# Modulation sums by ScalarE products and adding transfers, and a twentieth pair of FFN tiles by seven products

## The chip, the cores and the metric

One core of one Trainium2 chip. The metric is the device time of one execution in microseconds (us). Before the change three runs gave 699.42, 699.88 and 700.14; the median is 699.88.

## The reference, cut to what matters

One decoder layer in float32, sequence 512, width 1024. A conditioning vector c gives six modulation vectors, and two sublayers are each put back by a LayerNorm:

```python
c_act = silu(c)
mod = c_act @ ada_w + ada_b                       # [1024] x [1024, 6144]
sh1, sc1, g1, sh2, sc2, g2 = split(mod, 6)
h = x * (1 + sc1) + sh1
y = hybrid_mixer(h, ...)   # 8 attention heads and 16 SSD heads, one input and one output projection
x = layer_norm(ALPHA * x + (1 + g1) * y, ln1_g, ln1_b)
h = x * (1 + sc2) + sh2
u = causal_dwconv(h @ w_up, conv_w, conv_b)       # [512,1024] x [1024, 5632], conv of 3 taps
g, val = split(u, 2)
y = (silu(g) * val) @ w_down                      # [512,2816] x [2816,1024]
x = layer_norm(ALPHA * x + (1 + g2) * y, ln2_g, ln2_b)
```

## The kernel before, in words

The work is recorded by a list scheduler that lies in the kernel itself (class `Order`). Each piece of the layer is a Python generator, a "thread", that yields instructions, buffer requests (`Alloc`) and conditions (`Need`). `Order.run` holds a clock for each engine, prices each instruction (`price`), and always issues the instruction that could start first; among those that could start at nearly the same time, that of the thread with the lower priority number goes first. What it decides is only an order: on the chip each engine runs its own list strictly in order, and each instruction waits on semaphores for what it reads. A price or a delay (`late`) in the scheduler so changes no instruction, only where it stands. The engines are called PE (TensorE), DVE (VectorE, `V`), ACT (ScalarE, `A`), POOL (GpSimd, `G`), SP (SyncE, `S`, which issues the plain transfers); `GD` are transfers issued by POOL, which can add into their destination (`accum_op`).

**Products.** All products are float32 made of three fp32r products (high*high, high*low, low*high; `mm3`). Weights are loaded in 512 KB items (`raw`, by `w_load`), split by `w_split` into high and low parts (ACT copies `wh`, DVE subtracts to get `wl`), and used by `products()` in the order of the list `items`: input projection (tiles `fm`, `tm`), output projection (`po`, two halves of 512 columns), up projection of the FFN (`up` and `sP`), down projection (`dn`). `w_next` counts the items taken in `wpos[0]` and marks `("item", i)`; other threads start on that mark.

**Pairs of up tiles.** The up projection has 22 pairs of 128-column tiles (gate and value of one channel group). The first four tiles (pairs 0 and 1) are made in two halves of the sequence, since the first half is there sooner. A pair in the list `SEVEN` (line 695; pairs 3 to 21) is made by `seven(j)`: seven products of half-size blocks in place of eight, each of 12 matmuls of 256 columns, into two banks `sP`. `split_seven` makes its seven split weight blocks `wq` (DVE also sums two blocks, `sw`), `sums_seven` makes two of the sums by adding transfers on POOL (`raw<-raw`, `sw<-in_ffn_up_w`), and `seven_out` adds parts back on ACT and DVE. `quarters` makes the four sums `ts` of the activations that they need. Pair 2 is a plain pair: 48 matmuls of 512 columns.

**Modulation.** The first two of the six vectors (sh1, sc1) are made at the start. `ada_mid` makes g1 (`ada_row`, kept as a row in 128 partitions, used by `ln1`), then sc2 and sh2 (`ada_cols`, kept in `mcol`, used by `ln1_t`). `ada_last` makes g2 for the last LayerNorm. Each of the three in `ada_mid` calls `ada_acc`: eight loads `ad` of 128 rows of ada_w (512 KB each), each multiplied by a column of silu(c) (`csil`) and summed on DVE into `acc`, one load at the mark of one item. Then `ada_half` splits a half of `acc` (`acch`, `accl`) and sums it over the partitions by two matmuls (`pad`) with ones.

**The scan.** `dt_chain` writes the cumulated decays to DRAM (`drcs`), and `ssd_decay` reads them back for each of eight column tiles as a broadcast `csb` (512 KB, line 943 on). From it ACT makes `er` (exp of a 64x384 part, twice); POOL cuts the upper triangle (`affine_select`); ACT takes eight exps with a bias; DVE multiplies with the scores `sc`. PE reads the result in `py` (`ssd_out`); `ssd_state` makes states (`pst` on PE, `st` on ACT and DVE) and reads them by `pyo`.

**First LayerNorm.** `ln1` takes a 128-row tile of `po`, multiplies by g1 (`yp`), adds x (`xr`), takes statistics (`st`, `mv`; POOL takes the power -0.5), and scales to `XN`; `ln1_t` transposes it on PE (`pt`), applies `mcol` on ACT (`hk`) and splits to `h2h`, `h2l`.

All helpers record through line 309, so every row of the profile names L309; rows are told apart by their tiles.

## Time and profile before

| | |
|---|---|
| median of 3 runs | 699.88 us (699.42 to 700.14) |
| span of the profiled execution, first to last instruction | 698.53 us |
| what lies around the span (median less span) | 1.35 us |
| PE busy | 684.3 us, 98% |
| DVE busy | 607.3 us, 87% |
| ACT busy | 387.8 us, 56% |
| POOL busy | 103.4 us, 15% |
| granted TensorE clock, mean | 0.997 |
| transfers issued by SP, by POOL | 105.93 MB, 9.96 MB |

The page gives no time of its own for the profiled execution beside its span, so the span with the 1.35 us around it is taken for the median. A row of a timeline gives start, duration, engine, operation, `out<-in`, shape, count, and in brackets how long the engine had been idle and what ended that. Matmuls are pipelined and their ends are modelled: a 512-column matmul is drawn 0.39 us long and the next one starts about 0.23 us after it, so PE can be "busy" and still hide a wait of some 0.16 us.

### The profile page before, as it was taken

Reading aid. Unit: us, or ns where it says so; the run is one execution under the profiler, and the core shown is the slowest. Engines: PE = TensorE matmul, PEld = TensorE weight load, DVE = VectorE, ACT = ScalarE, POOL = GpSimd, SP = SyncE. Lnnn points to the kernel's source line nnn. Section 1 sums busy time; section 2 is a strip of 40 time slices with the busy share of each in tenths; the row PEclk is TensorE's granted clock in tenths of the full one; section 3 lists DMA queues with packets and bytes.
Section 4 is the critical chain, followed back from the end, with each engine's and each line's share of the span. In section 5 each row is a group of like instructions: output and inputs, shape, how many; then the busy total and the mean of one; then the engine's idle time right before and its main releaser. Section 6 shows DMA issues by size and latency. Waiting matters only on the chain.

```text
span 698.5 us, 11597 instructions
## 1 busy us (share of the span) xinstructions
PE 684.3 (98%) x4305; PEld 598.0 (86%) x4305; DVE 607.3 (87%) x1119; ACT 387.8 (56%) x739; POOL 103.4 (15%) x109
## 2 busy tenths in 40 slices
PE   8999999999999999999999999999999999999995
PEld 7787877888888888887898999999999998888885
DVE  5888989899999999889999999999999997357646
ACT  2437568845667545313886777777777776111300
POOL 0010021101000000000121121112222005910023
PEclk9999999999999999999999999999999999999998
DMA  8997074134455626677493787877897576232202
GB/s 269 308 289 241 16 215 149 37 87 126 120 178 160 237 92 212 246 275 256 137 233 73 174 200 165 187 174 167 189 204 173 130 255 220 94 108 70 91 30 92
DMA packets 134924, 116.64 MB, mean 167 GB/s; under 512 B 4565, under 2 KB 113489, under 8 KB 134867
## 3 DMA queue, kind: packets, MB, share of 16 engines
q1 hardware_dynamic: 122099, 105.93, 49.4%
q0 software_dynamic: 12768, 9.96, 9.8%
q8 instruction: 34, 0.56, 0.3%
q14 instruction: 23, 0.19, 0.1%
HBM read 106.66 MB, written 4.23 MB: 159 GB/s over the span
## 4 chain that ended last, share of the span: by engine, by line
PE 85%; DVE 6%; DMA 4%; SPq 3%; ACT 1%; issue 1%; POOL 0%; DVEq 0%; ACTq 0%; POOLq 0%
PE sP L309 27%; PE fm L309 18%; PE dn L309 18%; PE po L309 7%; PE first L309 3%; SPq L309 3%; PE tm L309 2%; PE psS L309 2%; PE pov L309 1%; PE pT L309 1%; PE py L309 1%; DMA csb<-drcs 1%; PE pyo L309 1%; PE up L309 1%; DMA raw<-in_ffn_up_w_dram 1%
## 5 line engine op out<-in xcount | busy, mean ns | idle before, releaser
L309 PE MATMUL sP<-ts,wq 128*128 128x256 f32 x912 | 113.9, 281 | 0.0
L309 DVE TENSOR_TENSOR wl<-raw,wh 128x1024 fp32r<-128x1024 f32 x64 | 80.6, 1265 | 36.6 <-ACT wh L309 36.1
L309 ACT ACTIVATE wh<-raw 128x1024 fp32r<-128x1024 f32 x64 | 67.3, 1055 | 78.0 <-PE dn L309 31.1
L309 PEld LDWEIGHTS sP<-ts,wq 128*128 128x128 f32 x912 | 110.4, 189 | 0.0
L309 PE MATMUL dn<-wh,mid 128*128 128x512 f32 (+1 forms) x356 | 102.7, 371 | 0.0
L309 PE MATMUL sP<-h2h,wq 128*128 128x256 f32 x456 | 87.2, 281 | 0.0
L309 PEld LDWEIGHTS dn<-wh,mid 128*128 128x128 f32 x356 | 64.7, 188 | 12.6
L309 PEld LDWEIGHTS sP<-h2h,wq 128*128 128x128 f32 x456 | 72.7, 189 | 0.0
L309 PE MATMUL fm<-hh,wh 128*128 128x512 f32 x176 | 72.6, 412 | 0.0
L309 PE MATMUL fm<-hh,wl 128*128 128x512 f32 x176 | 69.4, 394 | 0.0
L309 PE MATMUL fm<-hl,wh 128*128 128x512 f32 x176 | 69.4, 394 | 0.0
L309 PE MATMUL dn<-wl,mid 128*128 128x512 f32 (+1 forms) x178 | 66.1, 372 | 0.0
L309 PE MATMUL sP<-h2l,wq 128*128 128x256 f32 x228 | 64.0, 281 | 0.0
L309 DVE TENSOR_TENSOR wq<-raw,wq 128x512 fp32r<-128x512 f32 x76 | 50.8, 686 | 0.7
L309 ACT ACTIVATE wq<-raw 128x512 fp32r<-128x512 f32 x76 | 45.3, 623 | 0.0
L309 ACT ACTIVATE c<-sP 128x256 f32<-128x256 f32 x76 | 29.0, 382 | 28.5 <-PE sP L309 28.2
L309 PEld LDWEIGHTS sP<-h2l,wq 128*128 128x128 f32 x228 | 43.1, 189 | 0.1
L309 PE MATMUL po<-wh,os 128*128 128x512 f32 x128 | 42.1, 396 | 0.0
L309 PEld LDWEIGHTS fm<-hh,wl 128*128 128x128 f32 x176 | 33.1, 188 | 7.7
L309 PEld LDWEIGHTS fm<-hh,wh 128*128 128x128 f32 x176 | 33.2, 189 | 7.0 <-issue 0.7
L309 DVE TENSOR_TENSOR wq<-sw,wq 128x512 fp32r<-128x512 f32 x57 | 38.8, 684 | 0.0
L309 PEld LDWEIGHTS dn<-wl,mid 128*128 128x128 f32 x178 | 33.5, 188 | 6.2
(264 smaller groups left out, 1489.9 us busy)
## 6 DMA issues: line engine op xcount, KB each, us to landing
raw<-in_ffn_up_w_dram SPq DMA_DIRECT2D x44, 512.0 KB, 4.5
raw<-in_mix_in_w_dram SPq DMA_DIRECT2D x26, 512.0 KB, 5.8
ad<-in_ada_w_dram SPq DMA_DIRECT2D x24, 512.0 KB, 3.9
raw<-in_ffn_down_w_dram SPq DMA_DIRECT2D x22, 512.0 KB, 3.7
aw<-in_ada_w_dram SPq DMA_DIRECT2D x32, 256.0 KB, 5.8
raw<-in_mix_out_w_dram SPq DMA_DIRECT2D x12, 512.0 KB, 4.0
sw<-in_ffn_up_w_dram SPq DMA_DIRECT2D x19, 256.0 KB, 4.9
raw<-raw POOLq DMA_DIRECT2D x19, 256.0 KB, 4.6
```

What stands on the lines that cost most here:

```text
L309: getattr(self.hw[op.eng], op.fn)(*op.args, **op.kw)
```

## The change

- **Twentieth pair.** `SEVEN` begins at 2: pair 2 is made by seven products too.
- **Modulation sums.** In `ada_acc` the DVE multiply-adds go. ACT multiplies each load by its column of `csil` in place (the first one into `acc`), and seven adding transfers by POOL sum them into `acc`. This holds for g1, sc2 and sh2; `ada_last` still sums on DVE.
- **Loads ahead.** A thread `ada_load` of its own issues the 24 loads, up to two ahead of their use.
- **Priorities.** `ada_mid` goes from 3 (past item 16; 8 before that) to 1.9 (past item 8); `ada_last` goes from 8 to 2.6 eight items before the up projection.
- **Scheduler's prices.** A `csb` transfer counts as landing 1.0 us later for its readers; the 64x384 exp, the reciprocal and a large `affine_select` get other prices. Only the order follows from these.
- **A shared tile.** `OA` can be allocated by either of two attention threads.

```diff
-        self.regs[t.tensor.name].late = 2.0 if a.name == "ad" else 0.0
+        self.regs[t.tensor.name].late = {"ad": 2.0, "csb": 1.0}.get(a.name, 0.0)
...
-            return 0.04 + 0.00093 * n + (0.06 + 0.07 * ptr if ptr else 0) + (0.09 if "accum_out" in kw else 0)
+            return 0.04 + (0.0013 if outs[0].shape[0] == 64 and n == 384 else 0.00093) * n + (0.06 + 0.07 * ptr if ptr else 0) + (0.09 if "accum_out" in kw else 0)
...
-                return 0.065 + 0.0065 * n
+                return 0.15 + 0.0065 * n
...
-            return 0.06 + 0.001 * n + (0.5 if n > 512 else 0)
+            return 0.06 + 0.001 * n
...
-    SEVEN = list(range(3, 22))
+    SEVEN = list(range(2, 22))
...
-        if j % 2 == 0:
-            OA[j] = yield buf("e", [P, 2, 2, SEQ], "oa", dt=F32R)
+        if j - j % 2 not in OA:
+            OA[j - j % 2] = None
+            OA[j - j % 2] = yield buf("e", [P, 2, 2, SEQ], "oa", dt=F32R)
+            R.mark(("OA", j - j % 2))
+        yield Need(("OA", j - j % 2))
...
-    def ada_acc(idx, item):
+    ADQ = {}
+
+    def ada_load():
+        for idx, item in ((2, ADA0), (4, ADA1), (3, ADA2)):
+            for kc in range(KC):
+                yield Need(("item", item + kc))
+                aw = yield buf("b", [P, DM], "ad", "adraw")
+                yield S.dma_start(aw, ada[kc * P:(kc + 1) * P, idx * DM:(idx + 1) * DM])
+                ADQ[idx, kc] = aw
+                R.mark(("ad", idx, kc))
+
+    def ada_acc(idx):
         acc = yield buf("b", [P, DM], "acc")
         for kc in range(KC):
-            yield Need(("item", item + kc))
-            aw = yield buf("b", [P, DM], "ad", "adraw")
-            yield S.dma_start(aw, ada[kc * P:(kc + 1) * P, idx * DM:(idx + 1) * DM])
+            yield Need(("ad", idx, kc))
+            aw = ADQ.pop((idx, kc))
             if kc == 0:
-                yield V.tensor_scalar(acc, aw, csil[:, 0:1], None, op0=OP.mult)
+                yield A.activation(acc, aw, AF.Copy, scale=csil[:, 0:1])
             else:
-                yield V.scalar_tensor_tensor(acc, aw, csil[:, kc:kc + 1], acc, op0=OP.mult, op1=OP.add)
+                yield A.activation(aw, aw, AF.Copy, scale=csil[:, kc:kc + 1])
+                yield GD.dma_start(acc, aw, accum_op=OP.add)
             R.free(aw)
...
-    R.spawn(ada_mid(), lambda: 3 if wpos[0] > 16 else 8)
+    R.spawn(ada_mid(), lambda: 1.9 if wpos[0] > 8 else 8)
+    R.spawn(ada_load(), 4)
...
-    R.spawn(ada_last(), 8)
+    R.spawn(ada_last(), lambda: 2.6 if wpos[0] > UP0 - 8 else 8)
```

The lists of the engines differ from the start of the scan up to the start of the pairs by seven products; ahead of that and through the down projection they stand as before. Three places follow, each before and after the change.

ACT at the start of the scan, before: from the copy `csT` that feeds the decays' way through DRAM on. `wh` are weight copies, `Y` and `th` belong to the convolution, `er` and `csb` read the broadcast decays.

```order
L309 ACTIVATE csT_939<-pcs_929 64x128
...
L309 ACTIVATE th_951<-Y_659 128x512
L309 ACTIVATE wh_967<-raw_666 128x1024
L309 ACTIVATE er_985<-csb_962 64x384 x2
L309 ACTIVATE th_1010<-Y_659 128x512
L309 ACTIVATE er_987<-csb_963 64x384 x2
L309 ACTIVATE st_990<-pst_1021 128x128
L309 ACTIVATE wh_1023<-raw_809 128x1024
L309 ACTIVATE er_992<-csb_964 64x384 x2
L309 ACTIVATE csb_962<-csb_962,ncs_86 128x128 x8
```

The same engine and place after the change; `ad` is a product of the modulation, in place.

```order
L309 ACTIVATE csT_940<-pcs_930 64x128
...
L309 ACTIVATE th_952<-Y_659 128x512
L309 ACTIVATE wh_974<-raw_666 128x1024
L309 ACTIVATE ad_954<-ad_954,csil_75 128x1024
L309 ACTIVATE th_1016<-Y_659 128x512
L309 ACTIVATE wh_1024<-raw_809 128x1024
L309 ACTIVATE er_988<-csb_965 64x384 x2
L309 ACTIVATE er_990<-csb_966 64x384 x2
L309 ACTIVATE csb_965<-csb_965,ncs_86 128x128 x8
```

The product `ad`, the second `th` and the second `wh` now stand ahead of the first `er`; the copy `st` has left ACT (it is a copy on DVE now), and the first eight exps come after two `er` and not three.

POOL in the same stage, before: the triangle cuts of the column tiles.

```order
L309 AFFINE_SELECT csb_962<-csb_962 128x1024
L309 AFFINE_SELECT csb_963<-csb_963 128x1024
L309 AFFINE_SELECT csb_964<-csb_964 128x1024
L309 AFFINE_SELECT csb_1155<-csb_1155 128x1024
L309 AFFINE_SELECT csb_1193<-csb_1193 128x1024
```

And after; `DMA acc<-ad` are the adding transfers of the first modulation sum.

```order
L309 DMA acc_804<-ad_954 128x1024
L309 AFFINE_SELECT csb_965<-csb_965 128x1024
L309 AFFINE_SELECT csb_966<-csb_966 128x1024
L309 AFFINE_SELECT csb_967<-csb_967 128x1024
L309 DMA acc_804<-ad_1021 128x1024
L309 AFFINE_SELECT csb_1142<-csb_1142 128x1024
L309 AFFINE_SELECT csb_1177<-csb_1177 128x1024
L309 DMA acc_804<-ad_1104 128x1024
L309 AFFINE_SELECT csb_1248<-csb_1248 128x1024
```

Each adding transfer waits at the head of POOL's list for its product and for the landing of the one before it, and the cuts behind it wait with it.

DVE at the first tile of the first LayerNorm, before: from the product with g1 on. The rows `ISA junk` and `ISA col` are the column sums of sh2.

```order
L309 SCALAR_TENSOR_TENSOR acc_2836<-ad_3179,csil_75,acc_2836 128x1024
L309 TENSOR_TENSOR yp_3285<-po_3139,row_2286 128x512
L309 SCALAR_TENSOR_TENSOR xr_3031<-xr_3031,yp_3285 128x512
L309 BN_STATS st_3107<-xr_3031 128x6
L309 BN_AGGR mv_3108<-st_3107 128x2
L309 TENSOR_SCALAR mv_3108<-mv_3108 128x1
L309 ISA junk_3212,col_3211<-pad_3287,ident_68 128x128
...
L309 ISA col_3211 128x1
L309 SCALAR_TENSOR_TENSOR mv_3108<-mv_3108 128x1
```

And after:

```order
L309 SCALAR_TENSOR_TENSOR acc_2921<-ad_3256,csil_75,acc_2921 128x1024 x2
L309 TENSOR_TENSOR yp_3327<-po_3201,row_1678 128x512
L309 SCALAR_TENSOR_TENSOR xr_3098<-xr_3098,yp_3327 128x512
L309 BN_STATS st_3166<-xr_3098 128x6
L309 BN_AGGR mv_3167<-st_3166 128x2
L309 TENSOR_SCALAR mv_3167<-mv_3167 128x1
L309 TENSOR_TENSOR accl_3323<-acc_2921,acch_3322 128x512
L309 SCALAR_TENSOR_TENSOR mv_3167<-mv_3167 128x1
L309 TENSOR_SCALAR XN_3360<-xr_3098,mv_3167 128x512
```

Between the statistics and the scaling to `XN` one subtraction stands where the eight rows of the column sums stood; those come earlier now.

More of the change, by code (lines that the diff above doesn't have):

```diff
@@ L1107, in ada_half, with ada_row @@
         return pa
-    def ada_row(idx, key, res, item):
-        acc = yield from ada_acc(idx, item)
+    def ada_row(idx, key, res):
+        acc = yield from ada_acc(idx)
         row = yield buf("b", [P, DM], "row")
@@ L1122, in ada_cols @@
     def ada_cols():
-        for idx, item in ((4, ADA1), (3, ADA2)):
-            acc = yield from ada_acc(idx, item)
+        for idx in (4, 3):
+            acc = yield from ada_acc(idx)
             col = yield buf("t", [P, 8], "col")
@@ L1150, in ada_mid @@
         yield Need(("item", 2))
-        yield from ada_row(2, "g1p", ROWS, ADA0)
+        yield from ada_row(2, "g1p", ROWS)
         yield from ada_cols()
```

## The prediction

> **What bounds the kernel now.** I read the page first, then the busy time by stages, then the chain of waits and the timelines of the places where PE stands still. The page:
>
> ```profile
> span 698.5 us, 11597 instructions
> PE 684.3 (98%) x4305; PEld 598.0 (86%) x4305; DVE 607.3 (87%) x1119; ACT 387.8 (56%) x739; POOL 103.4 (15%) x109
> ```
>
> PE is busy for 98% of the span, so time can go in two ways only: less work on PE, or less idle time of PE. The stages show where it is idle (columns: PE, PEld, DVE, ACT, POOL busy, granted clock, DMA share, GB/s):
>
> ```profile
> core 0: us, PE busy (x) PEld busy (x) DVE busy (x) ACT busy (x) POOL busy (x), PEclk, DMA share, GB/s
> 0.00:20.00 20.00, 16.84 (x102) 14.91 (x103) 12.16 (x34) 6.57 (x12) 0.75 (x7) 1.00 0.93 273
> 20.00:40.00 20.00, 18.82 (x93) 14.61 (x92) 17.77 (x50) 8.03 (x14) 0.00 (x0) 1.00 1.11 314
> 40.00:60.00 20.00, 19.62 (x99) 15.15 (x99) 16.06 (x36) 11.74 (x17) 3.81 (x14) 1.00 0.97 309
> ...
> 80.00:100.00 20.00, 19.15 (x92) 15.16 (x91) 17.43 (x41) 10.50 (x20) 1.75 (x2) 1.00 0.51 152
> 100.00:120.00 20.00, 19.51 (x142) 15.61 (x140) 17.64 (x30) 17.71 (x50) 5.19 (x4) 1.00 0.53 166
> 120.00:320.00 200.00, 199.99 (x1134) 164.16 (x1133) 184.62 (x395) 107.79 (x223) 9.81 (x15) 1.00 0.50 162
> 320.00:340.00 20.00, 19.28 (x92) 15.35 (x91) 18.93 (x45) 11.19 (x25) 1.41 (x2) 1.00 0.52 176
> 340.00:380.00 40.00, 40.00 (x281) 37.06 (x280) 37.94 (x62) 30.91 (x55) 7.83 (x8) 1.00 0.73 171
> 500.00:520.00 20.00, 20.00 (x172) 20.00 (x171) 19.82 (x34) 14.82 (x29) 4.37 (x4) 1.00 0.83 186
> ```
>
> The first 60 us lose 4.7 us to the start loads, which the change does not touch; nor does it reorder the down projection and the tail. In between PE is idle for 0.85 and 0.49 us at the scan's start (80 to 120), 0.01 us from 120 to 320, and 0.72 us at the first LayerNorm (320 to 340): 2.07 us in all. That is everything a better order can give back. The chain that ended last says the same of the long stage:
>
> ```profile
> 380.76 187.56 PE sP L309 x1587
> 568.32 122.87 PE dn L309 x594
> ```
>
> Pairs by seven products run on PE without a break, 187.56 us for 1587 matmuls, though DVE is 99% busy beside them (19.82 of 20).
>
> **The change part by part.** *Twentieth pair.* The plain pair 2 lies between these starts:
>
> ```profile
> 367.64 0.40 PE L309 MATMUL up<-h2h,wh 128*128 128x512 f32 x1
> ...
> 378.80 0.28 PE L309 MATMUL sP<-h2h,wq 128*128 128x256 f32 x1
> ```
>
> Its 48 matmuls take 378.80 - 367.64 = 11.16 us. A pair by seven is 84 matmuls at 187.56/1587 = 118.2 ns, 9.93 us. Gain 1.23 us, on PE itself. Its cover: the activations' sums `ts` and the first blocks `wq` must be ready 11 us sooner than now.
>
> ```profile
> 350.50 1.04 PE L309 MATMUL pt<-ident,XN 128*128 128x128 f32 x8
> ...
> 364.13 0.69 DVE L309 TENSOR_TENSOR ts<-d,ts 128x512 fp32r<-128x512 f32 x1
> ...
> 368.98 0.68 DVE L309 TENSOR_TENSOR wq<-raw,wq 128x512 fp32r<-128x512 f32 x1
> ```
>
> PE gets from its last transposes (350.50) to the new pair's place in 17.1 us, and `ts` is done 14.3 us after them (364.8): 2.8 us of slack. The first `wq` now ends at 369.7, too late, but the new list of DVE has it and three more ahead of the `ts` rows; four operations of about 0.6 us apart eat most of the 2.8 us, and the subtractions of the plain pair that go and the modulation work that DVE loses give it back. I take 0, with 0 to 1 us lost as the bounds.
>
> *Modulation sums.* What DVE loses and ACT gains:
>
> ```profile
> L309 DVE SCALAR_TENSOR_TENSOR acc<-ad,csil,acc 128x1024 f32<-128x1024 f32 x28 | 35.7, 1280 | 0.3 <-DMA ad<-in_ada_w_dram 0.2
> L309 DVE TENSOR_SCALAR acc<-ad,csil 128x1024 f32<-128x1024 f32 x4 | 3.0, 745 | 0.0
> L309 ACT ACTIVATE wh<-raw 128x1024 fp32r<-128x1024 f32 x64 | 67.3, 1055 | 78.0 <-PE dn L309 31.1 <-DVE raw L309 23.3 <-PE po L309 15.7
> ```
>
> DVE is rid of 21 x 1.28 + 3 x 0.745 = 29.1 us; ACT gets 24 operations of the size of `wh`, 25.3 us. Nearly all of it lies between 85 and 300, where PE is idle for 0.01 us from 120 on: a freer DVE can give nothing there, and the 25 us on ACT cost nothing as long as it is not last (107.79 of 200 busy). At 100 to 120 ACT has 17.71 of 20, and there it can.
>
> *Adding transfers.* None of 512 KB is in the trace; the nearest rows are the adding ones of 256 KB, issued by POOL (last column: us to landing), beside the plain load:
>
> ```profile
> ad<-in_ada_w_dram SPq DMA_DIRECT2D x24, 512.0 KB, 3.9
> ...
> raw<-raw POOLq DMA_DIRECT2D x19, 256.0 KB, 4.6
> sw<-in_ffn_up_w_dram POOLq DMA_DIRECT2D x19, 256.0 KB, 6.4
> ```
>
> Half the bytes land in 4.6 us, so 4.6 is the low end and 9.2 (all of it growing with the bytes) the high one. I take 6.4, the slower of the two adding rows: the step is one product and one landing, 1.06 + 6.4 = 7.5 us. A step is due once per weight item:
>
> ```profile
> 192.65 0.38 SPq L309 DMA_DIRECT2D raw<-in_mix_in_w_dram  x1
> ...
> 217.61 0.38 SPq L309 DMA_DIRECT2D raw<-in_mix_out_w_dram  x1
> ```
>
> Four items start between these (192.65, 199.42, 208.43, 217.61): 8.3 us each. So the sums keep pace by 0.8 us a step; the point from which they fall behind is a landing of 7.2 us. [...] Behind each adding transfer wait the triangle cuts, attention's memsets and the powers on POOL; loads whose buffer held an `ad` wait for its landing on SP, and the weights behind them. For this coupling over 200 us without idle time I charge 0.1 us, bounds 0 and 4.
>
> *Start of the scan.* The chain here is the broadcast decays:
>
> ```profile
> 89.15 0.52 SPq L309 DMA_DIRECT2D raw<-in_mix_in_w_dram  x1
> 90.42 1.39 SPq L309 DMA_DIRECT2D csb<-drcs  x3
> ...
> 95.51 1.07 ACT L309 ACTIVATE er<-csb 64x384 f32<-64x384 f32 x2 [3.54 <-DMA csb<-drcs]
> ...
> 98.24 1.07 ACT L309 ACTIVATE er<-csb 64x384 f32<-64x384 f32 x2 [1.00 <-DMA csb<-drcs]
> ...
> 99.66 1.27 PE L309 MATMUL pyo<-CT,st 128*128 128x128 f32 x5 [0.85 <-ACT st L309]
> ...
> 101.67 7.14 ACT L309 ACTIVATE csb<-csb,ncs 128x128 f32<-128x128 f32 x24
> ...
> 105.39 0.69 DVE L309 TENSOR_TENSOR csb<-csb,sc 128x512 f32<-128x512 f32 x1 [0.52 <-issue]
> ...
> 111.69 0.88 PE L309 MATMUL py<-csb,xd 128*64 128x128 f32 x12 [0.47 <-issue]
> ```
>
> Before, ACT waits 3.54 and 1.00 us for the decays to land, the copy `st` queues behind that, and PE idles 0.85 us in `pyo`. Now `st` is on DVE and `pyo` comes six `tm` matmuls later (1.4 us): that wait goes. But one more load of 512 KB goes out ahead of the decays; at the 314 GB/s of 20 to 40 that is up to 1.7 us, so the second decay lands at 99 to 100. The product `ad` waits on ACT for that load, with `th`, `wh` and `er` behind it. The second `er` (1.07 us) and eight exps (7.14/24 = 0.3 us each) then end at about 102.5 to 103.5 and DVE's product (0.69 us and the way to it) 0.9 us later, while `py` is reached on PE at about 102.9: 98.8 without the wait, and 4.1 us for the six `tm`, nine more, `pyo` and `pst`. The `pyo` behind it waits in turn for an `st` that stands behind these products on DVE. So 0 to 2.3 us of waiting stand against 1.32 now (0.85 + 0.47): -1.3 to +1.0. I take -0.2.
>
> *First LayerNorm.* PE's two waits are for `XN`, at 0.41 and 0.31 us:
>
> ```profile
> 329.43 0.44 PE L309 MATMUL pt<-ident,XN 128*128 128x128 f32 x2 [0.41 <-DVE XN L309]
> ...
> 334.99 0.30 PE L309 MATMUL pt<-ident,XN 128*128 128x128 f32 x1 [0.31 <-DVE XN L309]
> ```
>
> The column sums of sh2 stood inside the first chain, on DVE; they are gone from it, as are half the multiply-adds around it. POOL's power is next. I take -0.5, bounds -0.7 and +0.5 (a POOL queue that is not free).
>
> *The rest* (prices, `OA`) acts through the order alone and is in the terms above.
>
> Sum on the profiled execution: 698.53 - 1.23 - 0.2 - 0.5 + 0.1 = 696.7. The median of the runs lies 1.35 above that span, so 699.88 - 1.83 = 698.05: **698.0 us**.
>
> **The rivals.** About 0.2% (1.4 us) is what a measurement of this kernel tells from no change, so faster means under 698.5 and slower over 701.3.
>
> *Every wait goes.* The extra microsecond for the decays does what it should and both stages run dry: 699.88 - 1.23 - 2.07 = 696.6. For it: DVE is 29 us freer. Against it: the later decays worked out above.
>
> *Only the pair counts.* The waits move and stay as large, or PE waits a microsecond at the first pair by seven: 699.88 - 1.23 + 0 to 1 = 698.7 to 699.7. For it: `py` seems to be reached before its exps are done, and `ts` has 2.8 us in hand at best.
>
> *The sums come late.* `pad` stands in PE's list at a fixed place and, if the last adding transfer has not landed, PE stops with everything behind it. From a landing of 7.2 us on the seven steps fall behind; at 9.2 us by 2 us each. If one sum of the three is late by two such lags, 4 us, the time is 702.0. For it: the high bound of the landing, and that POOL, SP and ACT are now tied together. Against it: the item spacing leaves 0.8 us a step at the landing that I take. [...]
>
> **How the numbers follow.** My forecast, with the pair and part of the waits, has a chance of 0.40, every wait gone 0.16: faster 0.56. Only the pair: 0.28, which is the same. Late sums: 0.16, slower. The predicted time is the forecast's, 698.0. The range goes from 696.0, just past the case with every wait gone, to 701.2, which takes in the third case and the cheaper half of late sums; some 0.15 is left out, most of it above.
>
> **What would show it.** In the changed profile: 1680 matmuls `sP` in one unbroken piece of about 198.5 us; no wait of PE at its first; ACT about 25 us busier and DVE about 25 us less (the twentieth pair gives some back); adding transfers `acc<-ad` landing in 5 to 7 us; idle time of PE of 1 to 1.5 us between 80 and 120 and under 0.3 at the LayerNorm. It is wrong if PE waits before `pad` or for weights between 120 and 320, if landing takes over 7.2 us, or if the piece of `sP` has gaps.

## The result, and the profile after

The changed kernel is slower. Its median of four runs is 706.12 us (705.22 to 709.83), beside 700.01 us of the kernel before on the same chip (699.42 to 701.01): a ratio of 1.0096, with a 95% interval of 1.007 to 1.0121. The prediction was 698.0 us, its range ended at 701.2. The profiled execution is the longest of the four, 709.83 us with a span of 707.66 and a mean granted clock of 0.991; the other three have spans of 703.1 to 704.4 and clocks of 0.996 to 0.998, and left no trace. Its first 60 us cost 0.9 us more than in the profile of before (`pd`, the first matmul behind the start, stands at 58.94 and not at 58.06). PE waits 1.84 us there for the first rows of x, where it waited 1.20, and the granted clock from 0 to 20 us is 0.91 where it was 1.00; the lists are the same there, so this is not the change.

The page of the changed kernel:

```profile
span 707.7 us, 11716 instructions
PE 689.1 (97%) x4341; PEld 602.5 (85%) x4341; DVE 589.6 (83%) x1121; ACT 408.4 (58%) x755; POOL 124.3 (18%) x132
```

DVE is 17.7 us less busy and ACT 20.6 us more, so the work did move. PE is busy for 4.8 us more, although the twentieth pair takes work from it: some matmuls must be slower. (Where they are is shown below.) The stages, with the columns of the prediction's table (PE, PEld, DVE, ACT, POOL, granted clock, DMA share, GB/s):

```profile
80.00:120.00 40.00, 40.00 (x241) 32.87 (x242) 36.78 (x81) 32.63 (x73) 9.44 (x8) 1.00 0.73 213
120.00:320.00 200.00, 193.70 (x1086) 156.09 (x1085) 160.81 (x389) 120.61 (x227) 25.71 (x33) 0.98 0.75 200
320.00:340.00 20.00, 20.00 (x87) 15.98 (x86) 16.59 (x21) 5.33 (x6) 2.36 (x3) 1.00 0.70 208
```

The two places where the change was to give time back are clean: no idle time at the start of the scan (1.34 us before) and none at the LayerNorm (0.72 before). The LayerNorm now begins behind 340 us, outside the last row; that PE does not wait there is told by its table of waits, which has no wait for `XN`. The 200 us between them, where PE stood still for 0.01 us before, now have 6.30 us of idle time, 48 matmuls less than before, and a clock of 0.98. The DMA share there went from 0.50 to 0.75.

Where the idle time lies is told by the lists that carry the sums. The adding transfers take this long from issue to landing (median; the shortest 4.4, the longest 9.9):

```profile
acc<-ad POOLq DMA_DIRECT2D x21, 512.0 KB, 7.6
```

That is above the 7.2 us that the prediction named as the point from which the sums fall behind. POOL's timeline shows them behind, in the third sum:

```profile
250.17 0.87 POOL L309 DMA_DIRECT2D acc<-ad  x1 [5.79 <-ACT wh L309]
...
259.35 0.93 POOL L309 DMA_DIRECT2D acc<-ad  x1 [1.62 <-DMA acc<-ad]
267.63 0.86 POOL L309 DMA_DIRECT2D acc<-ad  x1 [7.36 <-ACT os L309]
273.06 0.86 POOL L309 DMA_DIRECT2D acc<-ad  x1 [4.57 <-DMA acc<-ad]
283.52 0.86 POOL L309 DMA_DIRECT2D acc<-ad  x1 [9.60 <-DMA acc<-ad]
...
293.77 0.92 POOL L309 DMA_DIRECT2D acc<-ad  x1 [8.32 <-DMA acc<-ad]
```

Five steps from 250.17 to 293.77 make 8.7 us each, and what ends the wait is, in four of the five, the landing of the transfer before. The chain that ended last follows this sum to its end (start, length):

```profile
250.17 8.65 DMA acc<-ad
...
259.35 7.75 DMA acc<-ad
...
267.63 4.90 DMA acc<-ad
...
273.06 9.93 DMA acc<-ad
...
283.52 9.72 DMA acc<-ad
...
293.77 4.58 DMA acc<-ad
...
298.37 0.64 ACT acch L309
...
299.03 0.70 DVE accl L309
...
299.78 0.79 PE pad L309
```

Each of the five steps is one landing and 0.53 us more (250.17 + 8.65 + 0.53 = 259.35, and so on). PE stands before `pad` for 2.38 us (a row of PE's waits: total, times, longest):

```profile
PE pad L309 <- ACT acch L309: 2.4, 1, 2.4
```

The second sum does the same less directly. Its copy `acch` stands in ACT's list ahead of attention's rows, so these are late too, and PE waits 1.11 us in `fm` at 234.86 and 0.28 us at 237.97, both times for attention and not for the sum itself:

```profile
223.88 6.77 DMA acc<-ad
...
230.67 0.64 ACT acch L309
...
231.34 0.69 DVE accl L309
...
232.52 0.61 ACT pr L309 x2
```

The third place is SP. A load whose buffer held an `ad` waits for the landing of that `ad`, and with it everything behind it in SP's list (first the row of the table of SP's waits: total, times, longest; then SP's timeline):

```profile
SPq L309 <- DMA acc<-ad: 78.9, 12, 14.9
```

```profile
118.22 0.38 SPq L309 DMA_DIRECT2D raw<-in_mix_in_w_dram  x1
125.51 0.33 SPq L309 DMA_DIRECT2D ad<-in_ada_w_dram  x1
...
126.39 0.77 SPq L309 DMA_DIRECT2D fr<-in_ffn_conv_w_dram  x2
```

Between 118.60 and 125.51 SP issues nothing. Behind it stand the rows `fr` of the convolution's weights, which PE transposes next:

```profile
131.93 0.34 PE L309 MATMUL pf<-ident,fr 88*128 88x88 f32 x1 [2.00 <-DMA fr<-in_ffn_conv_w_dram]
131.99 0.77 PE L309 MATMUL fm<-hh,wh 128*128 128x512 f32 x1
132.56 0.63 PE L309 MATMUL fm<-hl,wh 128*128 128x512 f32 x1
132.99 0.63 PE L309 MATMUL fm<-hh,wl 128*128 128x512 f32 x1
...
135.95 0.40 PE L309 MATMUL fm<-hh,wh 128*128 128x512 f32 x1
136.19 0.40 PE L309 MATMUL fm<-hl,wh 128*128 128x512 f32 x1
```

Two things are to be seen here. PE waits 2.00 us. And then seven matmuls of 512 columns start 0.43 us apart (132.56 to 132.99) where such matmuls start 0.24 us apart at 135.95: about half the rate, for 3.4 us. The row of the stages has it as a lower granted clock:

```profile
120.00:140.00 20.00, 18.00 (x92) 14.42 (x91) 15.05 (x42) 14.14 (x33) 4.03 (x4) 0.91 0.71 160
```

In slices of 1 us the granted clock is 0.50 from 132 to 135 us. The same happens behind the wait before `pad`: 0.50 from 300 to 302 us, and less than 1 in the slices beside them. In this execution each of the two waits so costs 1.7 us more than its length (3.4 us at half the clock). The other three, with clocks of 0.996 to 0.998, can have had little of this: the profiles here that have no such slow stretch show 0.996 to 0.999.

In the last stage the pair does what it was meant to do. PE's timeline:

```profile
378.03 0.28 PE L309 MATMUL sP<-h2h,wq 128*128 128x256 f32 x1
...
381.64 1.58 PE L309 MATMUL sP<-ts,wq 128*128 128x256 f32 x11 [0.60 <-ACT c L309]
```

The chain from there on:

```profile
381.64 196.01 PE sP L309 x1656
577.65 122.39 PE dn L309 x591
```

From the first `sP` to the first `dn` it is 199.62 us, before 568.32 - 378.80 = 189.52: the pair takes 10.10 us in place of 11.16, with one wait of 0.60 us in it, for the first part `c` of ACT.

### The profile page after: what moved, and what is told of

Its sections match the earlier page's. It is cut to its first block, busy times and chain, and to the rows that moved or that the text cites. A ratio compares the mean times of both kernels' runs of the same rounds, so it can differ in the third digit from the quotient of the medians.

```text
span 707.7 us, 11716 instructions
## 1 busy us (share of the span) xinstructions
PE 689.1 (97%) x4341; PEld 602.5 (85%) x4341; DVE 589.6 (83%) x1121; ACT 408.4 (58%) x755; POOL 124.3 (18%) x132
## 4 chain that ended last, share of the span: by engine, by line
PE 80%; DMA 9%; DVE 6%; ACT 2%; issue 1%; SPq 0%; POOL 0%; DVEq 0%; ACTq 0%; POOLq 0%
PE sP L309 28%; PE dn L309 17%; PE fm L309 12%; DMA acc<-ad 7%; PE po L309 6%; PE first L309 5%; PE tm L309 3%; PE py L309 1%; PE psS L309 1%; PE pT L309 1%; PE pst L309 1%; PE pov L309 1%; DMA xk<-in_x_dram 1%; DMA fr<-in_ffn_conv_w_dram 1%; PE pyo L309 1%
## 5 line engine op out<-in xcount | busy, mean ns | idle before, releaser
L309 PE MATMUL sP<-ts,wq 128*128 128x256 f32 x960 | 120.0, 281 | 0.6 <-ACT c L309 0.6
L309 PEld LDWEIGHTS sP<-ts,wq 128*128 128x128 f32 x960 | 116.0, 189 | 0.9 <-ACT c L309 0.8
L309 DVE TENSOR_TENSOR wl<-raw,wh 128x1024 fp32r<-128x1024 f32 x62 | 77.8, 1260 | 35.5 <-ACT wh L309 35.2
L309 PE MATMUL sP<-h2h,wq 128*128 128x256 f32 x480 | 91.7, 281 | 0.0
L309 PEld LDWEIGHTS sP<-h2h,wq 128*128 128x128 f32 x480 | 76.6, 189 | 0.0
L309 PE MATMUL sP<-h2l,wq 128*128 128x256 f32 x240 | 67.4, 281 | 0.0
L309 DVE TENSOR_TENSOR wq<-raw,wq 128x512 fp32r<-128x512 f32 x80 | 53.6, 685 | 0.1
L309 POOL DMA_DIRECT2D acc<-ad x21 | 18.6, 887 | 161.9 <-ACT ad L309 76.2
L309 POOL DMA_DIRECT2D sw<-in_ffn_up_w_dram x20 | 26.8, 1339 | 94.1 <-DVE u L309 52.1
L309 ACT ACTIVATE wq<-sw 128x512 fp32r<-128x512 f32 x60 | 37.0, 626 | 9.9 <-DVE sw L309 9.5
```

What stands on the lines that cost most here:

```text
L309: getattr(self.hw[op.eng], op.fn)(*op.args, **op.kw)
```

## The experiments

The theory after this reading, A: the adding transfers land too late, and that alone makes the loss, by way of PE waiting for late sums and of SP's list waiting for landings. The rivals: the work that ScalarE took over, the new order of the lists, the loads ahead, or the pair. Eighteen kernels were run, five rounds each, beside the kernel before on the same chip (medians of 699.7 to 700.4 us).

### The same lists, other transfers

These kernels keep the list of every engine of the changed kernel and change only what the 21 transfers do, at the one line of the scheduler that issues an instruction. The scheduler still counts them as before, so nothing else moves.

**Half the bytes.** The second 512 columns of the sums are left out.

```diff
-        getattr(self.hw[op.eng], op.fn)(*op.args, **op.kw)
+        getattr(self.hw[op.eng], op.fn)(*(a[:, :512] if op.cost > 3 and op.eng == "GD" else a for a in op.args), **op.kw)
```

> The changed kernel with every list of every engine as it is, word for word, but each of the 21 adding transfers moves 256 KB and not 512: the sums of the second 512 columns are left out. Theory A, the landing of the adding transfers is what costs: they land in about 4.6 us, the waits of PE at 131.9 (fr), 234.9 and 238.0 (behind the late sum) and 299.0 (pad) go, with 12.3 us of excess in the profiled run and some 8 in a run of the median: 696.5 to 698.5. Rival C, the work that ScalarE took over or the changed order of the lists costs: 705 to 707, nothing changes.

Measured: 697.57 us (697.28 to 698.40), ratio 0.9966 (0.9954 to 0.9978). The transfers land in 6.1 us, not in 4.6, and PE has no wait in the long stage (its row of the stages, and the row of the transfers):

```profile
120.00:320.00 200.00, 200.00 (x1134) 163.19 (x1133) 170.42 (x398) 123.30 (x228) 25.21 (x33) 1.00 0.66 185
```

```profile
acc<-ad POOLq DMA_DIRECT2D x21, 256.0 KB, 6.1
```

All of the loss goes, and 2.4 us more: ScalarE's products, the order, the loads ahead and the pair are all still there. So is POOL's time for issuing a transfer, 0.86 to 0.92 us behind the first one. SP still waits 41.5 us for landings here, with no wait of PE from it. A further rival, weights that load too slowly beside the adds, is not what stops PE in the changed kernel: its table of waits names no load of `raw`.

**Copies in place of adds.** The sums are left out; each modulation keeps its last product alone. The same bytes go the same way.

```diff
-        getattr(self.hw[op.eng], op.fn)(*op.args, **op.kw)
+        getattr(self.hw[op.eng], op.fn)(*op.args, **({} if op.cost > 3 and op.eng == "GD" else op.kw))
```

> The changed kernel with the same lists and the same 21 transfers of 512 KB from POOL's queue, but they copy and do not add: the sums are left out, each modulation keeps its last product alone. Theory A3, it is the adding (the destination is read too) that makes the landing long: 3 to 5 us to landing and 697 to 698.5, like half the bytes. Theory A4, any transfer of 512 KB between tiles from this queue takes as long beside the weights' loads: 7 us or more, 705 to 707.

Measured: 697.51 us (697.27 to 699.35), ratio 0.9971 (0.9960 to 0.9981). The time is theory A3's, the landing is not: 6.3 us in the median, though it begins at 2.9. The row of the transfers, and POOL's timeline in the third sum:

```profile
acc<-ad POOLq DMA_DIRECT2D x21, 512.0 KB, 6.3
```

```profile
255.23 0.53 POOL L309 DMA_DIRECT2D acc<-ad  x1 [3.88 <-DMA acc<-ad]
258.91 0.53 POOL L309 DMA_DIRECT2D acc<-ad  x1 [3.15 <-ACT ad L309]
266.90 0.53 POOL L309 DMA_DIRECT2D acc<-ad  x1 [7.47 <-DMA acc<-ad]
```

The transfers are still often waited for, but a step is short enough. So between a landing of 6.3 and one of 7.6 us lie 8.6 us of time, with the prediction's threshold of 7.2 between them. How much of the DMA engines an add takes is told by the queue's row (packets, MB, share of the 16 engines), here of the changed kernel, of the copies, and of the run with the pair alone, which has none of the 21:

```profile
q0 software_dynamic: 16464, 21.50, 18.1%
```

```profile
q0 software_dynamic: 16464, 21.50, 14.3%
```

```profile
q0 software_dynamic: 13440, 10.49, 10.3%
```

With the spans of 707.7, 695.2 and 705.8 us these are 128.1, 99.4 and 72.7 us of all 16 engines: (99.4 - 72.7)/21 = 1.3 us for a copy of 512 KB, (128.1 - 72.7)/21 = 2.6 us for an add. By this estimate, which takes the queue's other transfers to cost the same in the three runs, an add took twice the DMA time of a copy here. What fills the rest of the 7.6 us was not taken apart.

**Two halves.** Each adding transfer as two of 256 KB, one behind the other. Nothing is left out.

```diff
-        getattr(self.hw[op.eng], op.fn)(*op.args, **op.kw)
+        for h in ((slice(0, 512), slice(512, 1024)) if op.cost > 3 and op.eng == "GD" else (slice(None),)): getattr(self.hw[op.eng], op.fn)(*(a[:, h] if h.stop else a for a in op.args), **op.kw)
```

> The changed kernel with the same lists, but each adding transfer of 512 KB is issued as two of 256 KB, one behind the other: the same bytes, the same sums. Half the bytes gave 697.57 us. Theory A1, one long transfer is slow and two of them overlap: the second half lands in 5 to 6.5 us, 698 to 700. Theory A2, the bytes that are added set the landing: the second half lands in 7.5 us or more, and its issue takes another 0.9 us of POOL: 705 to 709.

Measured: 703.39 us (700.84 to 704.60), ratio 1.0042 (1.0027 to 1.0058), between the two theories. The halves land in 6.6 us (median; 3.2 to 9.6). In the profiled execution, one of the two fastest of its runs, no wait for a sum is left; the one for `fr` is:

```profile
131.23 0.27 PE L309 MATMUL pf<-ident,fr 88*128 88x88 f32 x1 [2.68 <-DMA fr<-in_ffn_conv_w_dram]
...
131.60 0.40 PE L309 MATMUL fm<-hl,wh 128*128 128x512 f32 x1
131.84 0.39 PE L309 MATMUL fm<-hh,wl 128*128 128x512 f32 x1
```

Cutting the transfer helps the sums by 2.7 us at the median; the bytes added, and the wait of 2.68 us for `fr`, stay.

**One sum at a time as copies** (the seven transfers of the first sum, or of the third).

```diff
-        getattr(self.hw[op.eng], op.fn)(*op.args, **op.kw)
+        getattr(self.hw[op.eng], op.fn)(*op.args, **({} if op.args[0].tensor.name.endswith("_804") else op.kw))
```

`_804` is the accumulator of the first sum; the third sum's is `_2608`.

> The changed kernel with the same lists; the 7 adding transfers of the first sum copy and do not add (that sum is left out), the other 14 add. Theory A, each sum causes its own wait: the wait for fr at 131.9, which stands behind SP's wait for the third transfer, goes with 3.4 to 4.2 us, the waits at 234.9 and 299 stay: 701.5 to 703. Rival J, the lateness is passed on and one later wait takes up what an earlier one gave back: 705 to 707.

> The changed kernel with the same lists; the 7 adding transfers of the third sum copy and do not add (that sum is left out), the other 14 add. Theory A: the wait before pad at 299 goes, with 2.4 us and the slow matmuls behind it 4 to 5.5 in the profiled run, 3 to 4 in the median; fr and 234.9 stay: 702 to 703.5. Rival J: 705 to 707.

Measured: 705.45 us (703.91 to 706.48) and 705.36 us (701.65 to 707.94). Both miss theory A's numbers at the median; rival J has them. In the run of the first sum the wait for `fr` falls to 0.66 us, as expected, but PE now waits 1.84 us for `dh` at 284.86. In the run of the third, the wait before `pad` is gone and `fr` keeps 2.03 us; its profile is of one of its fastest runs, and the slower ones have none; its seven runs spread over 6.3 us, so the median says little. As far as the runs show, the loss is not a sum of three parts that can be taken off one by one: it is gone when no sum adds, and most of it stays when two of the three still do. The wait for `dh` shows one place to which it moves.

### SP's list

`fr` is asked for earlier, so its loads stand ahead of the loads that wait for a landing. In the third kernel of this group the mark is item 8 in place of 6.

```diff
     def ffn_params():
-        yield Need("v")
+        yield Need(("item", 6))
...
-    R.spawn(ffn_params(), 8)
+    R.spawn(ffn_params(), 3.5)
```

> The changed kernel, but the rows of the convolution's weights (fr) are asked for six weight items after the start of the list and not after V, so that their loads stand ahead of the loads that wait for an adding transfer. Theory A (two parts: fr behind SP's waits, and late sums at pad): the wait before pf goes, with 3 to 4 us, the waits behind the late sums stay: 702 to 703.5. Rival G, the fr wait only comes first and the sums' lateness is paid later anyway: 705 to 707.

> Two cures of the changed kernel together: each adding transfer as two of 256 KB, and the loads of fr ahead of the loads that wait for a landing. Nothing is left out. Theory A: the one wait that was left in the run with two halves (2.8 us for fr) goes and the sums are in time: 698 to 700. Rival K, the re-made lists put new waits for the sums or for attention's products elsewhere: 701 or more.

> As the run with two halves and fr ahead (699.51), but fr is asked for after eight weight items and not six, so its loads stand behind one more load of a modulation row. Theory A, fr's place on SP is what matters and one place later is still early enough: 698 to 700, no wait at pf. Rival K, fr again waits behind a landing or the re-made lists put a wait elsewhere: 701 or more.

Measured: `fr` ahead alone 701.32 us (699.87 to 703.52), ratio 1.0020 (1.0007 to 1.0032); with two halves 699.51 us (697.30 to 700.81), ratio 0.9994 (0.9982 to 1.0005); with two halves and the later mark 700.61 us (699.16 to 704.59), ratio 1.0016 (1.0001 to 1.0032). No wait at `pf` is left in any of the three. The first saves 4.8 us of the changed kernel's 706.12, somewhat more than expected. More than the place of `fr` differs in it: SP waits 16.6 us for landings and not 78.9, and the adds land in 7.2 us. That SP's waits are the larger part of the loss at the median is likely by this, but not shown. What is left in it are waits of 1.4 us for `acch`, 0.5 for `accl` and 2.1 for attention's `mx`. With the later mark the time lies between theory A and rival K. With both cures and the mark at item 6 the long stage is nearly clean:

```profile
120.00:320.00 200.00, 199.75 (x1131) 162.62 (x1131) 171.81 (x398) 123.22 (x226) 40.77 (x47) 1.00 0.80 210
```

That is the fastest version of the changed kernel that computes everything. It equals the kernel before at the median; its fastest run, 697.30, is where the copies are, but its runs spread by 3.5 us. I found no version that beats the kernel before beyond its uncertainty.

### The pair without the sums

The kernel before with the twentieth pair. With that edit alone the scheduler's threads end up waiting for each other's buffers, so one kernel takes the last modulation's priority from the change as well, the other the microsecond for the decays.

```diff
-    SEVEN = list(range(3, 22))
+    SEVEN = list(range(2, 22))
...
-    R.spawn(ada_last(), 8)
+    R.spawn(ada_last(), lambda: 2.6 if wpos[0] > UP0 - 8 else 8)
```

> The kernel before with one thing of the change, the twentieth pair by seven products (and the last modulation's priority, without which the list cannot be made). Theory A, the sums of the changed kernel come late and the rest of the change is sound: the prediction's first term holds, -1.23 us, so 698.5 to 699.0. Rival B, the twentieth pair itself costs time because its activations are not ready: 700 or more, and a wait of PE at the first sP.

> The kernel before with the twentieth pair and the extra microsecond for the decays, the sums and every priority as before. From the runs so far the pair is worth 0.9 us; the prediction's terms for the start of the scan and for the pair give 698.0 to 699.2. Rival, the twentieth pair needs room on DVE ahead of the first LayerNorm, which only sums away from DVE give (with the last modulation's sums pulled ahead PE waited 5.8 us there): 703 or more, with a wait for XN.

Measured: 705.64 us (705.13 to 707.82), ratio 1.0081 (1.0067 to 1.0095), and 699.79 us (698.63 to 700.70), ratio 0.9998 (0.9989 to 1.0006). The first shows neither theory: 0.28 us at `sP`, but 5.8 us at the LayerNorm, since the last modulation's sums now stand there on DVE (a row of PE's waits):

```profile
PE pt L309 <- DVE XN L309: 5.8, 1, 5.8
```

In the second the stages are:

```profile
80.00:120.00 40.00, 40.00 (x248) 32.31 (x248) 36.71 (x79) 29.39 (x71) 6.58 (x6) 1.00 0.55 173
120.00:320.00 200.00, 199.66 (x1129) 163.59 (x1128) 189.38 (x408) 108.97 (x223) 11.16 (x15) 1.00 0.51 165
320.00:340.00 20.00, 18.74 (x89) 14.74 (x87) 14.96 (x26) 9.23 (x22) 4.51 (x4) 1.00 0.64 161
```

The extra microsecond for the decays clears the scan's start by itself (1.34 us). The LayerNorm loses 1.26 us where it lost 0.72, and the long stage 0.34. The median is that of the kernel before, lower than it by 0.1 us and not by the 0.7 to 1.9 expected.

### Other ways to make the sums

All of these have lists made anew, so each tells of its sums and of its lists together.

**On DVE again**, with the new priority and with the old one (3 in place of 1.9; the second diff is in that kernel alone):

```diff
-                yield A.activation(acc, aw, AF.Copy, scale=csil[:, 0:1])
+                yield V.tensor_scalar(acc, aw, csil[:, 0:1], None, op0=OP.mult)
...
-                yield A.activation(aw, aw, AF.Copy, scale=csil[:, kc:kc + 1])
-                yield GD.dma_start(acc, aw, accum_op=OP.add)
+                yield V.scalar_tensor_tensor(acc, aw, csil[:, kc:kc + 1], acc, op0=OP.mult, op1=OP.add)
```

```diff
-    R.spawn(ada_mid(), lambda: 1.9 if wpos[0] > 8 else 8)
+    R.spawn(ada_mid(), lambda: 3 if wpos[0] > 16 else 8)
```

> The changed kernel with the three modulation sums back on DVE (24 operations as before the change); loads ahead, priorities, prices, the later decays and the twentieth pair are kept. Theory A: no adding transfer, no late sum: 697.5 to 699.5. Rival D, the loads ahead and the new priorities push weights and decays back: 703 or more, with waits of PE between 120 and 320.

> The kernel with the sums back on DVE that took 716.8 us, but with the priority of the three modulations as before the change (3 and not 1.9); loads ahead stay. Theory F, with the new priority DVE stood before sums whose rows had not come, with attention's products behind them: now 698 to 702. Rival D, the loads ahead do it: 712 or more.

Measured: 716.84 us (716.57 to 720.78) and 706.66 us (706.46 to 708.78). Theory A's 697.5 to 699.5 failed: without one adding transfer the kernel was slower still. In the first, PE waits 5.8 us before `fm` for `qk` of DVE, with three multiply-adds of the sums in the 12 us ahead of it; in the second 4.05 us at 268.58 for `mx`. So the priority costs 10 us with the sums on DVE (theory F), but what is left is 706.66 and not F's 698 to 702: neither it nor rival D says why.

**A later landing in the plan** (2.5 us more in the scheduler's reckoning):

```diff
-            e = max(self.clock["DMA"], s + 2.5) + op.cost
+            e = max(self.clock["DMA"], s + 2.5) + op.cost + (2.5 if op.cost > 3 else 0.0)
```

> The changed kernel, but the planner expects each adding transfer of 512 KB to land 2.5 us later than it did (its plan then is near the 7.6 us measured). The same work; the lists differ, above all the places of pad. Theory A in its first form, a plan that trusts the landing too early: PE's waits before pad and behind the late sum go, 698 to 702. Rival E, the transfers tie POOL, SP and ScalarE together whatever the plan says: 704 to 708, with waits of PE for fr or weights still there.

Measured: 719.35 us (717.14 to 719.83). No wait before `pad` is left, as theory A says, but that is all that came true. PE waits 1.5 us for `fr`, 3.2 for `XN` at the LayerNorm, and now also 4.6 us in `up` for `h2h` of ACT and 4.2 in `sP` for `wq` of DVE, for neither of which it had waited.

**Two rows summed before the transfer; columns shared with DVE; two chains; two chains in halves.** In the order of the expectations: `summed_in_pairs` has ScalarE's product, DVE's multiply-add, nine adding transfers, and three load buffers in place of two; `split_columns` gives 512 columns to DVE; `two_chains_fr_ahead` sums even and odd rows apart and adds them on DVE; `two_chains_in_halves` cuts its transfers as well and has the later mark for `fr`. The main lines for two rows, shared columns, and two chains:

```diff
+            yield V.scalar_tensor_tensor(to, aw2, csil[:, kc + 1:kc + 2], to, op0=OP.mult, op1=OP.add)
...
+                yield GD.dma_start(acc[:, HS[0]], aw[:, HS[0]], accum_op=OP.add)
+                yield V.scalar_tensor_tensor(acc[:, HS[1]], aw[:, HS[1]], csil[:, kc:kc + 1], acc[:, HS[1]], op0=OP.mult, op1=OP.add)
...
+            to = odd if kc % 2 else acc
+                yield GD.dma_start(to, aw, accum_op=OP.add)
+        yield V.tensor_add(acc, acc, odd)
```

> The changed kernel with two rows of the modulation summed before the adding transfer (ScalarE's product of one, DVE's multiply-add of the other): 9 adding transfers of 512 KB and not 21, 12 multiply-adds of 1.28 us back on DVE. Theory A: a step is due every 16.6 us and lasts 1.1 + 1.3 + 7.6 = 10 us, so nothing is late: 697.5 to 700. Rival F, multiply-adds of priority 1.9 on DVE stand ahead of attention's products and wait for rows, as in the run with all sums on DVE (716.8): 705 or more.

> The changed kernel with the modulation's columns shared out: the first 512 by ScalarE's product and an adding transfer of 256 KB, the second 512 by DVE's multiply-add (about 0.7 us, 21 of them). Theory A: the transfers land as in the run with half the bytes (6.1 us) and nothing is late: 697.5 to 700. Rival F, multiply-adds of priority 1.9 on DVE stand ahead of attention's products and wait for rows: 705 or more.

> The changed kernel with each sum as two chains (even and odd rows, each with its own accumulator, added by DVE at the end) and the loads of fr ahead. A transfer then has two items, 16.6 us, to land; all bytes are added. Theory A, it is the length of the serial chain that makes the sums late: no wait at pad, 698 to 700. Rival K, the re-made lists put new waits elsewhere: 701 or more.

> All three cures: two accumulators a sum, each adding transfer in two of 256 KB, fr after eight items. Theory A, with 16.6 us for a landing and short transfers no sum can be late, and the run-to-run differences of the other versions go: 697.5 to 699, spread under 2 us. Rival K, DVE's extra addition of 1.2 us a sum and re-made lists put waits elsewhere: 701 or more.

Measured: 704.26 us (703.49 to 705.26), 702.90 us (702.18 to 703.69), 703.49 us (701.96 to 704.95) and 703.37 us (701.93 to 704.29). All four miss theory A's range and none is below the kernel before. The two kernels with two chains lie where rival K put them; the other two lie between theory A and rival F. Their largest waits in the long stage are 2.4 us for `pr` of ACT, 1.0 for `pr` of ACT, 1.2 for `pr` of DVE and 1.8 for `mx` of DVE: attention's softmax in each, not `pad`. That the lists and not the sums cost here is likely but was not taken apart.

**Adds on GpSimd** of 128x1024 in place of the transfers:

```diff
-                yield GD.dma_start(acc, aw, accum_op=OP.add)
+                yield G.tensor_add(acc, acc, aw)
```

> The changed kernel with each adding transfer replaced by an addition of 128x1024 on GpSimd (products on ScalarE stay): 21 adds, no landing, no transfer between tiles. The nearest rows are the triangle cuts of that size, 1.1 to 1.2 us each with one input; with two inputs up to 2.5. Theory A: a step is 1.14 + 1.2 to 2.5 us, far under the 8.3 us between items, and loads wait for no landing: 697 to 699.5. Rival H, adds of up to 2.5 us on POOL stand ahead of triangle cuts and of the powers, or slow DVE: 701 or more, with waits for csb or XN.

Measured: 721.65 us (720.45 to 722.51), ratio 1.0313 (1.0298 to 1.0328), the slowest of all. The time is rival H's, the waits are not the ones it named: PE's largest are 2.6 us for `z` and 2.6 for `xe`, both of DVE, and not for `csb` or `XN`. An add takes 2.41 us in the median of the 21 (2.37 to 3.26). Two rows of the timelines of POOL and DVE:

```profile
188.46 2.37 POOL L309 TENSOR_TENSOR acc<-acc,ad 128x1024 f32<-128x1024 f32 x1 [1.89 <-ACT ad L309]
```

```profile
188.56 2.69 DVE L309 TENSOR_TENSOR xe<-xd,dec 128x384 f32<-128x384 f32 x1
```

`xe` takes 0.58 us in the changed kernel and 2.69 here: it ends 0.4 us behind POOL's add. `wl` takes about 2.1 us in the mean of the seven that overlap an add (1.2 to 3.4), 1.29 in the other 55. The rows `st<-st,dtot,pst`, with one input from PSUM, are not slower there (0.275 and 0.274 us). So this `xe` and, in the mean, `wl` are slower beside POOL's adds in this run; the cause was not shown.

## Why the prediction was wrong, point by point

**What bounds the kernel** was right: PE is busy without a break but for waits, and only less work on PE or less idle time could count. The sentence behind it was too narrow: "2.07 us in all. That is everything a better order can give back" is true, but a worse order can take any amount, and the long stage with 0.01 us of idle time was treated as if it had cover.

**Twentieth pair**, -1.23 with 0 to 1 lost: 10.10 in place of 11.16 us, so -1.06, with one wait of 0.60 us at the first product by the sums. The bounds held it. It is not the wait that was foreseen (for `ts` or the first `wq`), but for `c` of ACT.

**Modulation sums**: ACT +20.6 us and DVE -17.7, smaller than the 25.3 and 29.1 of the working. That they cost nothing on ACT is shown by the copies: ScalarE has the same products there, at 697.51.

**Start of the scan**, -0.2 with -1.3 to +1.0: all of the 1.34 us of idle time is gone, in the changed kernel and in the run with the pair and the decays alone. The low bound was right; the working that put `py` ahead of its exps was not borne out. **First LayerNorm**, -0.5: 0.72 us gone in the changed kernel, 0.33 in the run with half the bytes and 0.72 in the copies. Right.

**Adding transfers** is the step that failed. Three numbers of it are wrong. "I take 6.4, the slower of the two adding rows": measured 7.6, on the wrong side of the prediction's own threshold of 7.2. Both rows came from the stage of the pairs by seven. Here the same 256 KB land in 6.1 us and copies of 512 KB in 6.3, in a stage whose DMA share the change itself raises from 0.50 to 0.75; so a median of 4.6, the lower bound, was out of reach for twice the bytes. And "For this coupling over 200 us without idle time I charge 0.1 us, bounds 0 and 4": measured 8.6 us, the distance from the changed kernel to the copies on the same lists. The third is the threshold of 7.2 itself. It took a step to be one product and one landing; in the third sum a step is one landing and 0.53 us, and the product is no part of it. With the 8.3 us between items the sums then fall behind from a landing of 7.8 us. The median of 7.6 lies under that, the five landings from 250.17 on lie over it, 8.2 in the mean. So the rival came true by a way a little other than the one written: the landings of that stretch were too long, and a threshold too low by 0.6 us pointed the right way. In these runs the copies of 512 KB took 2.9 us at the least and 6.3 at the median, the adds 4.4 and 7.6.

**The sums come late**, the rival with a chance of 0.16, is what happened, and at its place (`pad` at 299, 2.38 us). Its price of 702.0 was too low by 4 us, since it counted only the wait before `pad`. What it left out: SP's list, which waits 78.9 us for landings and brings `fr` late (named in the text, but charged only within the 0.1 us of the coupling and not in this rival; the version with `fr` ahead gains 4.8 us); ACT's and DVE's lists, where `acch` and `accl` stand ahead of attention; and, in the profiled execution, the slow matmuls behind a wait. Against the half of the bytes the profiled execution loses 707.66 - 696.17 = 11.5 us: 0.9 in the first 60 us, 6.3 in idle time of the long stage, 3.4 by the granted clock behind the waits at 132 and 299 (two stretches of 3.4 us at 0.50, 1.7 us each), and 0.9 that I cannot place. At the median, where the loss is 8.6 us, the clocks of the runs leave little room for the third of these; that it is nearly all waits there is argued, since those runs left no trace.

**What would show it** did its work: of the marks of failure that were named, a wait before `pad` and a landing over 7.2 us are found, and the wait for `fr`, rows of the convolution's weights, fits the third, a wait for weights between 120 and 320. With landings in time, the forecast's other terms sum to what was said: predicted 698.0, and 697.5 to 697.6 measured on the same lists, with part of the sums left out.

**Open**: how the loss divides between the three sums (taking one out gave 0.7 us, all three 8.6), and why versions with all bytes added scatter by 2.4 to 5.4 us from run to run. That the landings of a run decide it is argued from the waits, not shown. The cause is shown for the lists of the changed kernel: versions with the sums on DVE, without one adding transfer, were slow too, on lists of their own, and why is open.

## What to carry to other kernels

Where a step repeats at nearly the pace at which it is due, do not take a middle value for its one unknown duration: look on which side of the break-even point it will fall, and measure it in the stage where it will run, with the traffic that the change adds. A transfer in place of an engine's add freed the engine here (DVE by 17.7 us) but made a landing out of it, of 7.6 us in the median; ask which queues then wait for that landing (the buffer's next load on SP, the consumer's list), and price each of them. To find the cost of one part in a kernel whose order a scheduler makes, keep the lists and change only the instruction; the thirteen versions here with lists made anew lie between 699.5 and 721.7 us, and it was two of the five with the same lists, half the bytes and the copies, that showed the cause.

## What the runs showed of the hardware that was not expected

**Matmuls at half rate behind a wait.** Behind waits of PE of 2.00 and 2.38 us in the changed kernel the matmuls of the next 3.4 us start 0.43 us apart in place of 0.24, at a granted clock of 0.50. It is not a matter of the length alone: behind 2.68 us in the run with two halves the next ones start 0.24 us apart, and behind 2.03 us in the run with the third sum as copies there is no sign of it (mean granted clocks of these two executions 0.996 and 0.997, of the kernel before 0.997). What brings it on, and what makes it 3.4 us long, is not shown by these runs.

**An add took twice the DMA engines' time of a copy** of the same 512 KB between tiles: 2.6 and 1.3 us of all 16, by the estimate worked out above.

**POOL's issue of an adding transfer took longer**: 0.86 to 0.93 us, beside 0.53 to 0.59 for a copy of the same shape (the first of each kernel took longer, 1.06 and 0.76). It did not go by the bytes: the adds of 256 KB took 0.86 to 0.92 too.
